# How the first gated per-layer input gets the low parts of its weights: a subtraction on GpSimd in place of a negative on ScalarE and an adding transfer

## The chip, the cores and the metric

The kernel runs on one core of a Trainium2 chip. The metric is the device time of one execution in microseconds, the median over several runs. Lower is better. The profile is one profiled execution, whose rows the prediction quotes.

## The reference

A two-layer decoder trunk over 512 tokens of 1024 features, all in float32. Each layer has a half-step SwiGLU, a token mixer (retention in layer 0, forgetting attention in layer 1), a second half-step SwiGLU, and then a gated per-layer input. The last of these is what the change touches:

```python
for i in range(DEPTH):
    nw = norm_w[i]
    h = h + 0.5 * swiglu(rmsnorm(h, nw[0]), ffn_w_in[i, 0], ffn_w_out[i, 0])
    hn = rmsnorm(h, nw[1])
    h = h + (retention(...) if i % N_MIXERS == 0 else forgetting_attention(...))
    h = h + 0.5 * swiglu(rmsnorm(h, nw[2]), ffn_w_in[i, 1], ffn_w_out[i, 1])
    gate = jax.nn.sigmoid(rmsnorm(h, nw[3]) @ ple_w_gate[i])
    h = h + gate * (p[i] @ ple_w_proj[i])
return rmsnorm(h, final_norm_w)
```

## The kernel before

The hidden state h lies in SBUF, transposed, as eight blocks of 128 features by 512 tokens. Every product is made of three TensorE products in a rounded type (fp32r): high part of the weight with high part of the input, high with low, low with high. TensorE's order is written out by hand; the order of the instructions on ScalarE (ACT), VectorE (DVE), GpSimd (POOL) and SyncE (SP, which issues the loads) is made by a planner from the program's order, its own durations and the buffers that are free. Each of these engines then works through its list in order.

**Weights.** All weight tiles stand in one list (W.plan). take() hands out the next one and first makes those up to two further ahead (LOOKAHEAD). A tile's making: SP loads 512 KB into one of four raw buffers (wraw); ScalarE copies it, rounded, to the tile's high half; the low half is raw minus high. There are three tiles (wpool), so a new one can only be written when TensorE has left an older one. For the low half there are two ways, chosen by W.low when a tile is made:

- an engine: ScalarE's copy (L82), then a subtraction on that engine (L83), VectorE's or GpSimd's;
- None: ScalarE's copy (L120), ScalarE's negative of the raw tile into the low half (L121), and a transfer that reads the weights from memory again and adds them to it (L122). The transfer is issued from GpSimd's queue, and the raw buffer is free after the negative.

The feed-forwards do most of their input weights in pairs (Strassen's scheme). Of a pair's quarters, sums are made on VectorE (L151) and split (L82, L83); the first half of a pair and one of its quarters get their low parts by negative and adding transfer whatever W.low is. The first two weight pairs of a feed-forward are done plainly (plain(), L524), and their halves are ordinary tiles of the list.

**The gated input, ple().** In layer 0 it is done in one part of 512 tokens (parts is 1), in layer 1 in two. For each of the eight blocks m there are a gate product (gates(), through proj() and mm3(), L312 to L314: 24 matmuls) and a projection (added(): 6 matmuls), each in a PSUM bank of its own. rest(m) then multiplies the gate by the norm's row (L1106, VectorE), takes the sigmoid (L1107, ScalarE), multiplies by the projection (L1110) and adds to h (L1111). nxt.block(m) follows: it prepares the block for the next feed-forward's norm, in quarters for the pairs (quarters(): scaled copies L381 and L396 and rounded parts L376 and L384 on ScalarE, differences L388, L406, L411, L412 and low parts L377 and L385 on VectorE; four more splits L305 and L306) and squares it (L428, L432).

The list is here: projection tile, five gates, the second projection tile, three gates, and then the next feed-forward's two plain pairs as four tiles. As tiles are made two ahead, the projection's first tile and the first gate are made before ple() sets W.low, and the feed-forward's first two tiles are made inside it, at the last two gates. W.low is set back to VectorE at the end of ple(). One projection tile is held over four blocks, so the gates have the other two tiles between them.

Of the kernel before, what the change touches and what calls it, by code (L numbers as in the profile page):

```python
# [187 lines left out]
def trunk(ctx, tc, a):  # L188
    nc = tc.nc
# [15 lines left out]
    W = Weights(tc, wraw, wpool)  # L205
# [81 lines left out]
    def bank():  # L287
        return psum.tile([P, S], F32, name="bank")

    def temp(dtype=F32):  # L290
        return tmp.tile([P, S], dtype, name="tmp")
# [19 lines left out]
    def mm3(out, wh, wl, xh, xl, first, last):  # L311
        nc.tensor.matmul(out, wh, xh, start=first, stop=False)  # L312
        nc.tensor.matmul(out, wh, xl, start=False, stop=False)  # L313
        nc.tensor.matmul(out, wl, xh, start=False, stop=last)  # L314
# [159 lines left out]
    def proj(srcs, n, out=None, cols=slice(0, S), take=W.take):  # L474

        ws = [take(s) for s in srcs]
        os = out or [bank() for _ in ws]
        for k in range(KB):
            ks = slice(k * P, (k + 1) * P)
            for o, (wh, wl) in zip(os, ws):  # L480
                mm3(o, wh[:, ks], wl[:, ks], n.hi[k][:, cols], n.lo[k][:, cols], k == 0, k == KB - 1)
        return os
# [581 lines left out]
    def ple(l, n, nxt, phi, plo, parts=1):  # L1064

        w = S // parts
        with ExitStack() as pools:
# [7 lines left out]
            def weights(src):  # L1075
                if id(src) not in ws:
                    ws[id(src)] = W.take(src)
                return ws[id(src)]

            for part in range(parts):  # L1080
                ts_ = slice(part * w, (part + 1) * w)

                both = {}

                def half(m, i):

                    if parts == 1:
                        return bank()
                    if m not in both:
                        both[m] = bank()  # L1090
                    return both[m][:, i * w : (i + 1) * w]

                def gates(ms):
                    return proj([ple_g[l][m] for m in ms], n, [half(m, 1) for m in ms], ts_, weights)

                def added(m):
                    wp = weights(ple_p[l][m // 4])
                    o = half(m, 0)
                    for k in range(2):
                        ks = slice(((m % 4) * 2 + k) * P, ((m % 4) * 2 + k + 1) * P)  # L1100
                        mm3(o, wp[0][:, ks], wp[1][:, ks], phi[k][:, ts_], plo[k][:, ts_], k == 0, k == 1)
                    return o

                def rest(m, g, o):
                    t1, t2, hm = temp()[:, :w], temp()[:, :w], h[m][:, ts_]
                    nc.vector.tensor_tensor(out=t1, in0=g, in1=n.r[:, ts_], op=ALU.mult)  # L1106
                    nc.scalar.activation(t1, t1, AF.Sigmoid)  # L1107
                    if parts > 1 and m == KB - 1:
                        nc.scalar.activation(warm, t1[:, 0:1], AF.Sqrt)
                    nc.vector.tensor_tensor(out=t2, in0=o, in1=t1, op=ALU.mult)  # L1110
                    nc.vector.tensor_tensor(out=hm, in0=hm, in1=t2, op=ALU.add)  # L1111
                    if parts == 1:
                        nxt.block(m)
                    else:
                        nxt.new = m == 0
                        nxt.square(m, ts_, keep=m == KB - 1)
                        nc.gpsimd.tensor_scalar(out=hm, in0=hm, scalar1=fw[:, m : m + 1], scalar2=None, op0=ALU.mult)

                m = 0
                if part == 0:  # L1120
                    W.low = None if parts == 1 else nc.gpsimd
                    os = [added(m) for m in range(2 + parts)]
                    gs = gates((0,)) if parts == 1 else gates((0, 1, 2, 3))
                    n.columns()
                    m = len(gs)
                    gs += gates((m,))
                    n.rows()
                    if parts == 1:
                        os += [added(3)]
                        rest(0, gs[0], os[0])  # L1130
                        gs += gates((2,))
                        rest(1, gs[1], os[1])
                        gs += gates((3,))
                    for m in range(2 if parts == 1 else 0, 4):
                        rest(m, gs[m], os[m])
                    m = 4
                    if parts > 1:
                        rest(4, gs[4], added(4))
                        m = 5
                while m < KB:  # L1140
                    g = gates((m,))[0]
                    rest(m, g, added(m))
                    if part > 0 and m == 2:
                        diag = final_scale(nxt, slice(ts_.start - w, ts_.start))
                    if part > 0 and m == 4:
                        final(diag, slice(ts_.start - w, ts_.start))
                    m += 1
# [4 lines left out]
    def final_scale(n, ts_):  # L1152

        w = ts_.stop - ts_.start
        nb = w // P
        totals = [bank() for _ in range(nb)]
        for i, t in enumerate((n.acc[:, ts_], n.kept)):
            for j in range(nb):
                nc.tensor.matmul(
                    totals[j][:, 0:2], t[:, j * P : (j + 1) * P], ones[:, 0:2], start=i == 0, stop=i == 1  # L1160
                )
        r, v, t = (stat.tile([P, nb], F32, name=x) for x in ("last", "cv2", "ct2"))
        for j in range(nb):
            mean_eps(v[:, j : j + 1], totals[j][:, 0:1])
        rsqrt(r, v, t)
        diag = temp()[:, :w]
        nc.vector.tensor_tensor(
            out=diag.rearrange("p (j t) -> p j t", j=nb), in0=ident.unsqueeze(1).to_broadcast([P, nb, P]),
            in1=r.unsqueeze(2).to_broadcast([P, nb, P]), op=ALU.mult,
        )  # L1170
        return diag

    def final(diag, ts_):
        w = ts_.stop - ts_.start
        rows, copy = bank()[:, :w], temp()[:, :w]
        nc.tensor.matmul(rows, ones, diag, start=True, stop=True)
        nc.scalar.copy(copy, rows)
        ov = a["outT"].rearrange("(b p) t -> p b t", p=P)
        for b in range(KB):
            hb = h[b][:, ts_]  # L1180
            if b < 2:
                nc.gpsimd.tensor_tensor(out=hb, in0=hb, in1=copy, op=ALU.mult)
            else:
                nc.vector.tensor_tensor(out=hb, in0=hb, in1=rows, op=ALU.mult)
        for b0, b1, eng in ((2, 4, nc.sync), (4, 6, nc.scalar), (0, 2, nc.scalar), (6, 8, nc.sync)):
            eng.dma_start(out=ov[:, b0:b1, ts_], in_=hall[:, b0:b1, ts_])
# [142 lines left out]
```

## Time and profile before

| | |
|---|---|
| median of 3 runs | 2228.97 us (2226.98 to 2231.87) |
| span of the profiled execution, first to last instruction | 2230.5 us |
| TensorE busy | 2154.5 us, 97% |
| VectorE, ScalarE, GpSimd busy | 1447.1, 1212.3, 450.7 us |
| moved by transfers | 272.33 MB |
| granted TensorE clock, mean | 0.987 |

Of the profiled execution the page gives the span; its own time from outside isn't listed apart from the three runs, and the span lies within their spread. The gated input of layer 0 runs from about 1126 to 1193 us of the span, the next feed-forward's plain part till about 1230.

How to read the rows. In a timeline a row is: start, duration, engine, line, operation, written tile and what it reads, shapes, count; in brackets the engine's idle time before it and what ended that. PE is TensorE, PEld its weight load; L12 is line 12 of the kernel. The end of a matmul is modelled: each row lasts longer than the distance to the next. A row of waits names who waited for whom: total us, times, longest. The chain that ended last is followed back from the end, and its rows are start, duration, what. In a row of windows stand the stretch, its length, then busy time and instructions of PE, PEld, DVE, ACT and POOL, granted clock, share of the transfer engines, GB/s. A row of transfers ends with KB each and us from issue to landing. A row of groups by tile or line gives count, shortest, median and longest in ns, and the first and last start.

### The profile page before, as it was taken

To read this page: it belongs to the slowest core of one execution; us is meant where nothing else is said; L and a number is where in the kernel's file an instruction comes from. 1 tells how busy PE (TensorE), PEld (TensorE's weight loads), DVE (VectorE), ACT (ScalarE), POOL (GpSimd) and SP (SyncE) were. 2 spreads that over 40 slices of the span, in tenths; PEclk is the share of its full clock that TensorE was granted. 3 is DMA by queue.
4 is the path that set the end of the run, shared out by engine and by line. 5 is a ranking of instruction groups with operands and counts; after the bars stand their busy time and mean duration, and the time that the engine had idled before them with its cause. 6 is when DMAs were issued, how large, how long until landed. Compare 5 with 4: busy or idle time off the path is not lost.

```text
span 2230.5 us, 34455 instructions
## 1 busy us (share of the span) xinstructions
PE 2154.5 (97%) x13525; PEld 1937.5 (87%) x13525; DVE 1447.1 (65%) x2631; ACT 1212.3 (54%) x2037; POOL 450.7 (20%) x352
## 2 busy tenths in 40 slices
PE   7999999999999999999997999999999999999998
PEld 7999997888888798989876989898788888999987
DVE  8686776352542776767746677675675686777764
ACT  7565553433233663735555646364786775555543
POOL 0010003444444010101110001012334200110154
PEclk9999999999999999999998999999999999999999
DMA  5465563232222254746464457373622244655631
GB/s 176 113 163 150 138 161 95 81 99 76 88 83 76 85 137 119 170 133 152 129 151 117 114 136 182 113 167 103 153 91 87 69 116 112 159 158 137 152 104 39
DMA packets 86755, 272.33 MB, mean 122 GB/s; under 512 B 9520, under 2 KB 13104, under 8 KB 86592
## 3 DMA queue, kind: packets, MB, share of 16 engines
q1 hardware_dynamic: 63328, 209.78, 28.7%
q0 software_dynamic: 22032, 59.25, 15.9%
q8 instruction: 106, 1.74, 0.3%
q10 hardware_dynamic: 1232, 1.09, 0.1%
q14 instruction: 57, 0.47, 0.1%
HBM read 267.96 MB, written 2.13 MB: 121 GB/s over the span
## 4 chain that ended last, share of the span: by engine, by line
PE 80%; DVE 7%; ACT 6%; DMA 4%; issue 3%; POOL 0%; SPq 0%; DVEq 0%; ACTq 0%; POOLq 0%
PE bank L493 29%; PE bank L314 14%; PE bank L312 13%; PE bank L313 13%; PE bank L524 3%; DMA wraw<-in_ffn_w_in 3%; PE bank L678 2%; PE bank L679 2%; PE bank L680 2%; DVE w L83 1%; DMA w<-in_ple_gate 1%; DVE sums L151 1%; ACT p L982 1%; ACT w L82 1%; DVE tlo L303 1%
## 5 line engine op out<-in xcount | busy, mean ns | idle before, releaser
L82 ACT CAST w<-wraw 128x1024 fp32r<-128x1024 f32 (+1 forms) x232 | 235.1, 1021 | 431.0 <-PE bank L314 252.6
L314 PE MATMUL bank<-unit_a,w 128*128 128x512 f32 x736 | 288.9, 393 | 12.7 <-DMA w<-in_ple_gate 8.4
L312 PE MATMUL bank<-unit_a,w 128*128 128x512 f32 x736 | 289.8, 394 | 1.9 <-ACT w L82 1.6
L313 PE MATMUL bank<-unit_a,w 128*128 128x512 f32 x736 | 287.9, 391 | 0.2 <-DVE unit_a L303 0.2
L82 ACT CAST s<-sums 128x512 fp32r<-128x512 f32 x320 | 191.2, 617 | 155.3 <-DVE sums L151 106.6
L314 PE MATMUL bank<-unit_d,w 128*128 128x512 f32 (+1 forms) x712 | 268.1, 377 | 4.6 <-DVE w L83 4.6
L312 PE MATMUL bank<-unit_d,w 128*128 128x512 f32 (+1 forms) x712 | 269.2, 378 | 3.2 <-ACT w L82 1.6
L313 PE MATMUL bank<-unit_d,w 128*128 128x512 f32 (+1 forms) x712 | 268.3, 377 | 1.8 <-DVE unit_d L303 1.8
L83 DVE TENSOR_TENSOR s<-sums,s 128x512 fp32r<-128x512 f32 x320 | 213.7, 686 | 81.4 <-ACT s L82 80.4
L83 POOL TENSOR_TENSOR w<-wraw,w 128x1024 fp32r<-128x1024 f32 x83 | 202.6, 2445 | 233.5 <-ACT w L82 223.4
L122 POOL DMA_DIRECT2D a<-in_ffn_w_in x80 | 70.1, 876 | 651.4 <-ACT a L121 444.8
L83 DVE TENSOR_TENSOR w<-wraw,w 128x1024 fp32r<-128x1024 f32 (+1 forms) x149 | 175.8, 1185 | 28.3 <-ACT w L82 27.7
L493 PE MATMUL bank<-unit_b,s 128*128 128x256 f32 x880 | 185.9, 278 | 0.0
L493 PE MATMUL bank<-unit_d,s 128*128 128x256 f32 x1140 | 179.2, 277 | 0.0
L314 PEld LDWEIGHTS bank<-unit_a,w 128*128 128x128 f32 x736 | 138.8, 189 | 45.5 <-DMA w<-in_ple_gate 10.1
L493 PE MATMUL bank<-unit_a,s 128*128 128x256 f32 x1260 | 176.1, 277 | 1.9 <-ACT unit_a L376 1.1
L585 DVE SCALAR_TENSOR_TENSOR tmp<-bank,rows 128x512 f32<-128x512 f32 x96 | 66.0, 689 | 165.3 <-PE bank L314 164.0
L312 PEld LDWEIGHTS bank<-unit_a,w 128*128 128x128 f32 x736 | 139.0, 189 | 32.4 <-ACT w L82 3.5
L313 PEld LDWEIGHTS bank<-unit_a,w 128*128 128x128 f32 x736 | 139.0, 189 | 28.8 <-DVE unit_a L303 0.5
L493 PEld LDWEIGHTS bank<-unit_a,s 128*128 128x128 f32 x1260 | 158.8, 188 | 2.7 <-ACT unit_a L376 1.6
L314 PEld LDWEIGHTS bank<-unit_d,w 128*128 128x128 f32 x712 | 134.4, 189 | 30.5 <-DVE w L83 6.6
L312 PEld LDWEIGHTS bank<-unit_d,w 128*128 128x128 f32 x712 | 134.5, 189 | 30.3 <-ACT w L82 3.3
(270 smaller groups left out, 4801.1 us busy)
## 6 DMA issues: line engine op xcount, KB each, us to landing
wraw<-in_ffn_w_in SPq DMA_DIRECT2D x174, 512.0 KB, 4.3
wraw<-in_ffn_w_out SPq DMA_DIRECT2D x64, 512.0 KB, 4.7
w<-in_ffn_w_in POOLq DMA_DIRECT2D x58, 512.0 KB, 5.5
a<-in_ffn_w_in POOLq DMA_DIRECT2D x80, 256.0 KB, 6.2
wraw<-in_ffn_w_out SPq DMA_DIRECT2D x32, 384.0 KB, 3.7
wraw<-in_ret_qk SPq DMA_DIRECT2D x16, 512.0 KB, 3.5
wraw<-in_ret_v SPq DMA_DIRECT2D x16, 512.0 KB, 3.6
wraw<-in_ret_g SPq DMA_DIRECT2D x16, 512.0 KB, 3.5
```

The lines of the kernel that those rows point to most:

```text
L82: self.nc.scalar.copy(hi, raw)
L83: self.low.tensor_tensor(out=lo, in0=raw, in1=hi.bitcast(F32), op=ALU.subtract)
L122: self.nc.gpsimd.dma_start(out=lo, in_=src, accum_op=ALU.add)
L312: nc.tensor.matmul(out, wh, xh, start=first, stop=False)
L313: nc.tensor.matmul(out, wh, xl, start=False, stop=False)
L314: nc.tensor.matmul(out, wl, xh, start=False, stop=last)
L493: add = lambda w, x, start, stop: nc.tensor.matmul(out, w, x, start=start, stop=stop, skip_group_check=True)
L524: nc.tensor.matmul(o[:, HALVES[t]], x[:, ks], y, start=k == t == q == 0, stop=k == KB - 1 and q == 2, skip_group_check=True,)
L585: nc.vector.scalar_tensor_tensor(out=t1, in0=o, scalar=-0.5, in1=n.r, op0=ALU.mult, op1=ALU.mult)
L678: nc.tensor.matmul(os[t], xh, wh[:, js], start=k == 0, stop=False)
L679: nc.tensor.matmul(os[t], xh, wl[:, js], start=False, stop=False)
L680: nc.tensor.matmul(os[t], xl, wh[:, js], start=False, stop=k == KB - 1)
```

## The change

One line of ple() changes. In the first part of the gated input W.low becomes GpSimd in both layers; in layer 1 it already was.

```diff
                 m = 0
                 if part == 0:
-                    W.low = None if parts == 1 else nc.gpsimd
+                    W.low = nc.gpsimd
                     os = [added(m) for m in range(2 + parts)]
```

For the tiles made while that holds in layer 0, split() goes from the second way to the first: no negative on ScalarE, no transfer issued from GpSimd's queue, but a subtraction of 128x1024 on GpSimd, which reads the raw buffer and the high half. The tiles, the matmuls and their order on TensorE stay.

## The prediction

> **What bounds the kernel now.** I read, in this order: the head of the page; what TensorE waits for around the first gated input (1095 to 1225 us); the timeline of each engine there; the chain that ended last in the same place.
>
> ```profile
> span 2230.5 us, 34455 instructions
> PE 2154.5 (97%) x13525; PEld 1937.5 (87%) x13525; DVE 1447.1 (65%) x2631; ACT 1212.3 (54%) x2037; POOL 450.7 (20%) x352
> PE bank L524 <- DMA w<-in_ffn_w_in: 9.3, 1, 9.3
> PE bank L314 <- DMA w<-in_ple_gate: 8.4, 4, 3.5
> ```
>
> TensorE bounds the program and idles for 76 us in all; 17.7 us of that are here, and both waits are for transfers that the change removes. Time can come only out of these idles or out of a slow clock, and be lost only as new idles. The timeline of TensorE shows the five gaps, of 0.47, 1.02, 3.37, 3.55 and 9.25 us:
>
> ```profile
> 1145.28 0.50 PE L314 MATMUL bank<-unit_a,w 128*128 128x512 f32 x1 [0.47 <-DMA w<-in_ple_gate]
> 1152.03 0.50 PE L314 MATMUL bank<-unit_a,w 128*128 128x512 f32 x1 [1.02 <-DMA w<-in_ple_gate]
> 1167.95 0.50 PE L314 MATMUL bank<-unit_a,w 128*128 128x512 f32 x1 [3.37 <-DMA w<-in_ple_gate]
> 1185.39 0.50 PE L314 MATMUL bank<-unit_a,w 128*128 128x512 f32 x1 [3.55 <-DMA w<-in_ple_gate]
> 1186.66 0.51 PE L313 MATMUL bank<-unit_a,w 128*128 128x512 f32 x1
> 1190.30 0.40 PE L313 MATMUL bank<-unit_a,w 128*128 128x512 f32 x1
> 1203.50 3.15 PE L524 MATMUL bank<-unit_b,w 128*128 128x256 f32 x13 [9.25 <-DMA w<-in_ffn_w_in]
> 1209.68 1.26 PE L524 MATMUL bank<-unit_c,w 128*128 128x256 f32 x6
> ```
>
> Between 1186.66 and 1190.30 ten matmuls take 3.64 us, where undisturbed ones start 0.227 apart (0.23 in the chain's rows below): the clock was halved after the 3.55 us gap, which costs 3.64 - 2.27 = 1.4 us. The rows from 1203.50 are half-rate too at first.
>
> The last gap is the largest, but the chain says that it isn't what sets the end of this place:
>
> ```profile
> 1191.85 0.23 PE bank L313
> ...
> 1192.34 1.05 ACT w L120
> ...
> 1199.13 0.62 ACT a L120
> 1199.75 0.54 ACT tmp L1107
> ...
> 1209.08 0.34 DVE tmp L412
> 1209.42 0.61 DVE unit_c L377
> 1210.03 0.04 issue
> 1210.08 1.94 PE bank L524 x14
> ```
>
> Here the reader sees ScalarE and VectorE, not the transfer: TensorE, released at 1203.50, reaches the norm's last block (unit_c) at 1209.68 and finds it just being split. Had the low part come at once, TensorE would still have stood at unit_c till 1210.0. So the 9.25 us gap alone is worth about 0.3 us. What starts that chain is the copy at 1192.34, which waits for gate 7 to leave its weight tile.
>
> **The change, part by part.** Which tiles: the ones emitted while W.low is None.
>
> ```profile
> L120 ACT CAST w<-wraw x10: 1042/1054/1057, 1126.7 to 1192.3; 128x1024 fp32r<-128x1024 f32 x10
> L121 ACT ACTIVATE w<-wraw x10: 1042/1048/1057, 1127.7 to 1193.9; 128x1024 fp32r<-128x1024 f32 x10
> 1192.34 1.05 ACT L120 CAST w<-wraw 128x1024 fp32r<-128x1024 f32 x1 [4.98 <-PE bank L314]
> 1195.25 0.87 POOL L122 DMA_DIRECT2D w<-in_ffn_w_in  x1 [11.39 <-ACT w L121]
> w<-in_ffn_w_in POOLq DMA_DIRECT2D x1, 512.0 KB, 8.2
> w<-in_ple_gate POOLq DMA_DIRECT2D x7, 512.0 KB, 7.3
> L83 POOL TENSOR_TENSOR w<-wraw,w x83: 2359/2392/3631, 367.8 to 2168.2; 128x1024 fp32r<-128x1024 f32 x83
> ```
>
> Ten tiles: seven gates, one projection, and the first two of the next feed-forward (call the last one B). Removed: ten negatives of 1.05 us on ScalarE, ten issues of 0.87 on GpSimd, ten adding transfers of 7 to 8 us. Added: ten subtractions of 2.39 us on GpSimd (up to 3.63 in disturbed places). The copies stay. From the copy's start to the low part in place: before, for B, 1195.25 + 8.2 - 1192.34 = 11.1 us; after, 1.05 + 2.39 = 3.4, at most 4.7.
>
> *Gate stalls: gone, -10.9 us.* A gate's tile comes free two weights earlier; TensorE then has a projection (6 matmuls), a gate (24) and a projection (6) before the third matmul of the tile, 36 x 0.227 = 8.2 us. 11.1 doesn't fit into that (3.37 and 3.55 missing), 4.7 does with 3.5 to spare for a copy late in ScalarE's queue. The gaps sum to 8.41; start to start each loses 0.16 more (a matmul's row lasts 0.39, the next starts after 0.227) and 0.11 in the restart (0.34 to the next), 4 x 0.27 = 1.1; and the half clock's 1.4 goes. Gate 7 then ends, and B's copy could start, at 1192.34 - 10.9 = 1181.4.
>
> *B's low part: 9.25 becomes about 2 us.* TensorE needs it some 2 us after gate 7 (a projection of 1.4, five matmuls); it comes 3.4 to 4.7 after. By the chain above this is covered by the norm: nothing.
>
> *What is late next: the elementwise chain, +4.8 us.* From B's copy to unit_c it takes 1210.03 - 1192.34 = 17.7 us, whatever TensorE does. It would move by the full -10.9 if VectorE kept up. But a VectorE instruction with both inputs in SBUF stands still beside a GpSimd subtraction, as the retention stage shows:
>
> ```profile
> 472.31 0.68 DVE L698 TENSOR_TENSOR tmp<-bank,sin 128x512 f32<-128x512 f32 x1
> 472.91 2.91 DVE L700 TENSOR_TENSOR tmp<-tmp 128x512 f32<-128x512 f32 x1
> 472.88 2.39 POOL L83 TENSOR_TENSOR w<-wraw,w 128x1024 fp32r<-128x1024 f32 x1 [0.69 <-ACT w L82]
> 1095.00:1193.00 98.00, 89.59 (x390) 72.84 (x389) 49.37 (x81) 53.13 (x77) 18.45 (x16) 0.98 0.55 135
> ```
>
> 2.91 for 0.68: 2.2 us lost to one subtraction; an instruction that reads a PSUM bank (L698) or falls into a gap loses nothing. So a subtraction costs the chain 0 to 2.2 us. The Trainium skill says the same on its page "SBUF — State Buffer", section "SBUF: two separate sides": VectorE with two SBUF inputs and GpSimd hold one pair of ports as an exclusive lock, for the whole instruction. The rows here agree with it; by that rule taken at its worst the change is the slow rival below.
>
> VectorE is half busy here (49.37 of 98 us), so the early subtractions (gates 2 to 6, the projection) I cost at nothing: the chain there waits for TensorE's banks, with ScalarE idle up to 4.98 ahead of a copy. Without that cover they would cost six times 0 to 2.2. The three of gate 7 and the two feed-forward tiles stand where VectorE next splits the norm's blocks from SBUF (L377, L388, L406): three times 1.6, between the half of 2.2 and the whole, is 4.8. The lowest is 0, the highest nine times 2.2 = 19.8. The first of the ten, at 1127.7, has the last squares' sum behind it on GpSimd, and after that:
>
> ```profile
> 1131.96 0.69 DVE L303 TENSOR_TENSOR tmp<-acc,tmp 128x512 fp32r<-128x512 f32 x1 [1.86 <-ACT tmp L302]
> 1135.97 0.95 PE L326 MATMUL bank<-ones_r,tmp 128*128 128x2 f32 x8
> ```
>
> 1135.97 - 1131.96 - 0.69 = 3.3 us of cover, against 2.39 - 0.87 = 1.5 more on GpSimd: nothing (without the cover 1.5).
>
> *ScalarE:* ten negatives gone, 10.5 us of 53 busy; off the chain but for the one at 1193.92, whose place the subtraction takes. *SP's queue:* a raw buffer comes free when the subtraction, no longer the negative, has read it. B's raw buffer carries the next pair's load, and ScalarE's L120 at 1199.13 waits for that:
>
> ```profile
> 1193.92 1.04 ACT L121 ACTIVATE w<-wraw 128x1024 fp32r<-128x1024 f32 x1
> 1194.99 4.12 DMA wraw<-in_ffn_w_in
> wraw<-in_ple_gate SPq DMA_DIRECT2D x16, 512.0 KB, 3.5
> 1201.10 0.88 POOL L122 DMA_DIRECT2D a<-in_ffn_w_in  x1 [4.97 <-ACT a L121]
> ```
>
> Free 3.4 us after the copy's start instead of 2.6: +0.9; the load without an adding transfer beside it 3.5 instead of 4.1: -0.6. I take +0.3; ends 0 and +0.9. *GpSimd's queue:* behind B's subtraction stands only the next pair's adding transfer, issued at 1201.10 before; nothing.
>
> *The clock, +1.7 us.* TensorE, early at unit_c, waits there in pieces for up to 10 us, and the row at 1186.66 shows what follows a gap of 3.55: 3.4 us at half rate, 1.7 lost. Before, the same loss (from 1203.50) lay under the chain. Ends: 0 (pieces too short) and 3.4 (two such stretches). The Trainium skill's page "TensorE: Matmul & The Clock Gate", section "Part 1: The HAM clock gate (the "warmup" mystery)", gives a free-running window of 3413 ns for it; the trace's 3.4 us agrees, and by that rule the term is one window, as taken.
>
> **Sum:** -10.9 + 4.8 + 0.3 + 1.7 = -4.1 us, against a span of 2230.5; the time outside the span isn't shown. The span lies 1.5 us above the median of the runs (2228.97), so the median becomes 2224.9, or 0.18% less. A measurement of this kernel tells about 0.2% (4.5 us) from no change: the forecast lies just at that edge.
>
> **Rivals.**
>
> ```profile
> 1231.04 1.23 DVE L83 TENSOR_TENSOR w<-wraw,w 128x1024 fp32r<-128x1024 f32 x1 [6.99 <-ACT w L82]
> ```
>
> *The norm keeps up, gain of 9 to 11.* Subtractions fall beside PSUM reads, or the planner, which orders ScalarE, VectorE and GpSimd anew, puts the pair sums (L151, L83, 4 to 5 us of VectorE inside the 17.7) behind the norm's last block. For it: half-busy VectorE. Against: the next stage has little to give, since the 6.99 us of idle VectorE in this row are the slack in which postponed sums can be made before the first block with pairs. -10.9 + 0.3 + 1.7 or less: 2218 to 2220.
>
> *Hidden anyway, no change.* The elementwise chain turns out to be paced by itself from gate 2 on: the early subtractions cost too, and together all nine take about 1 us each, 9.2 in all, which with 0.3 + 1.7 is the 10.9 that the gates gain. 2227 to 2231.
>
> ```profile
> 2155.15 6.21 POOL L83 TENSOR_TENSOR w<-wraw,w 128x1024 fp32r<-128x1024 f32 x2
> 2155.66 3.43 DVE L83 TENSOR_TENSOR w<-wraw,w 128x1024 fp32r<-128x1024 f32 x1
> ```
>
> *Slower: the shared ports.* All nine stand in VectorE's way, at 1.6 each: 14.4 + 0.3 + 1.7 - 10.9 = +5.5, 2234.5; at 2.2 each 2240. It decides from 1.0 us per subtraction on the chain. For it: in the last stage two subtractions beside a busy VectorE took 3.1 each (the first row), and VectorE's own 3.43 for the 1.23 of the row at 1231.04. Against: here VectorE has half its time free, and a late block only matters once TensorE has used up its banks.
>
> *Does it do what it says?* Yes: split() with GpSimd as W.low always subtracts; pairs keep their own adding transfers.
>
> **How the numbers follow.** Forecast 0.45 (its own range 2220 to 2229), norm keeps up 0.25, hidden 0.16, slower 0.14. Faster by over 0.2% (below 2224.5): the 0.25 and not quite half of the forecast's, 0.45; within 0.2%: 0.40; slower: the 0.14 and a little of what the new order may spoil elsewhere, 0.15. Range: from between the forecast and the full gain, 2216, to the slower rival's 2234; outside lie about 2 in 10.
>
> **What would show it.** Right: no wait for w<-in_ple_gate; ten more L83 subtractions on GpSimd at 2.4 to 3.1; gate 7 ends near 1181; TensorE's new wait before 1205 names VectorE's L377 or L385; VectorE's two-SBUF rows stretched to 1.5 to 2.9 from 1140 on; unit_c near 1204 to 1206. Wrong: TensorE still waiting for low parts (then copies are stuck in ScalarE's queue); unit_c at 1199 or before (locks cheap); waits in gates 3 to 7 for banks or copies (locks everywhere); or the difference arising after 1250, where the change touches nothing but the planner's order.

## The result, and the profile after

The changed kernel takes 2217.13 us (median of 4 runs, 2215.84 to 2218.95), the one before 2228.15 beside it: ratio 0.9944, 95% interval 0.9928 to 0.9961. Two repetitions gave 0.995 (0.9934 to 0.9966) and 0.9948 (0.9929 to 0.9968). Over all runs of this study the mean is 12.1 us lower (16 runs against 111, standard error 0.9). The forecast was -4.1.

The head of the profile after, and GpSimd's group of subtractions between 1110 and 1215 us:

```profile
span 2214.2 us, 34442 instructions
PE 2148.7 (97%) x13525; PEld 1933.3 (87%) x13525; DVE 1459.4 (66%) x2631; ACT 1203.1 (54%) x2027; POOL 466.8 (21%) x352
L83 POOL TENSOR_TENSOR w<-wraw,w 128x1024 fp32r<-128x1024 f32 x10 | 24.9, 2493 | 39.6 <-ACT w L82 35.6 <-issue 4.0
```

Ten subtractions of 2.5 us have come, ten negatives and ten adding transfers have gone. What TensorE waits for between 1095 and 1245 us:

```profile
PE bank L524 <- ACT w L82: 5.7, 1, 5.7
PE bank L524 <- POOL w L83: 2.4, 1, 2.4
PE bank L493 <- ACT tmp L545: 2.3, 1, 2.3
PE bank L524 <- ACT unit_c L376: 1.2, 1, 1.2
PE bank L524 <- DVE w L83: 0.7, 1, 0.7
PE bank L524 <- DVE unit_c L377: 0.4, 1, 0.4
```

No wait for a gate's weights is left. In their place stands one of 5.7 us for a copy that the forecast didn't have. TensorE's timeline there (start, duration, what, wait):

```profile
1182.17 0.51 PE L524 MATMUL bank<-unit_b,w 128*128 128x256 f32 x3
1188.34 0.80 PE L524 MATMUL bank<-unit_b,w 128*128 128x256 f32 x2 [5.66 <-ACT w L82]
1191.54 3.14 PE L524 MATMUL bank<-unit_b,w 128*128 128x256 f32 x13 [2.40 <-POOL w L83]
1199.88 0.38 PE L524 MATMUL bank<-unit_c,w 128*128 128x256 f32 x1 [1.18 <-ACT unit_c L376]
1200.69 0.86 PE L524 MATMUL bank<-unit_c,w 128*128 128x256 f32 x5 [0.43 <-DVE unit_c L377]
```

In the kernel before it was:

```profile
1193.50 0.75 PE L524 MATMUL bank<-unit_b,w 128*128 128x256 f32 x5
```

So the plain feed-forward starts 11.3 us earlier (1182.17 for 1193.50); unit_c is reached at 1199.88 instead of 1209.68. ScalarE's list tells why tile B is late, VectorE's what the locks do:

```profile
1182.70 0.72 ACT L396 ACTIVATE tmp<-hall,small 128x512 f32<-128x512 f32 x1 [3.06 <-DVE hall L1111]
1187.26 1.03 ACT L82 CAST w<-wraw 128x1024 fp32r<-128x1024 f32 x1
1165.88 2.79 DVE L1111 TENSOR_TENSOR hall<-hall,tmp 128x512 f32<-128x512 f32 x1
1179.87 2.80 DVE L1111 TENSOR_TENSOR hall<-hall,tmp 128x512 f32<-128x512 f32 x1
1189.20 2.58 DVE L306 SCALAR_TENSOR_TENSOR unit_a<-hall,small,unit_a 128x256 fp32r<-128x256 f32 x1
1199.95 0.69 DVE L377 TENSOR_TENSOR unit_c<-tmp,unit_c 128x512 fp32r<-128x512 f32 x1
```

Before, ScalarE stood 4.98 us at the copy of B (1192.34) with L396 of block 6 behind it. The planner has now put block 6's instructions (L396 at 1182.70) ahead of that copy, so the copy starts only at 1187.26, though gate 7 ended near 1180.8. VectorE's two-input rows of 0.69 and 0.48 us stretch to as much as 2.8 beside a subtraction; the excesses of its nine stretched rows sum to 12.1 us. Ahead of the first split of unit_c VectorE's list had seven sums and subtractions of the feed-forward's weights (L151, L83) before. The planner has now put three of them, pair sums of 1.8 us, behind it. Their rows, first in the kernel before (unit_c split at 1209.34), then after (split at 1199.95):

```profile
1202.12 1.29 DVE L83 TENSOR_TENSOR s<-sums,s 128x512 fp32r<-128x512 f32 x2
1207.13 0.68 DVE L151 TENSOR_TENSOR sums<-sums,wraw 128x512 f32<-128x512 f32 x1
1207.73 0.68 DVE L151 TENSOR_TENSOR sums<-wraw 128x512 f32<-128x512 f32 x1
1202.09 0.69 DVE L83 TENSOR_TENSOR s<-sums,s 128x512 fp32r<-128x512 f32 x1
1203.29 0.69 DVE L151 TENSOR_TENSOR sums<-sums,wraw 128x512 f32<-128x512 f32 x1
1203.89 0.68 DVE L151 TENSOR_TENSOR sums<-wraw 128x512 f32<-128x512 f32 x1
```

### The profile page after: what moved, and what is told of

It reads as the page before. It is cut to its first block, busy times and chain, and to the rows that moved or that the text cites. A ratio compares the mean times of both kernels' runs of the same rounds, so it can differ in the third digit from the quotient of the medians.

```text
span 2214.2 us, 34442 instructions
## 1 busy us (share of the span) xinstructions
PE 2148.7 (97%) x13525; PEld 1933.3 (87%) x13525; DVE 1459.4 (66%) x2631; ACT 1203.1 (54%) x2027; POOL 466.8 (21%) x352
## 4 chain that ended last, share of the span: by engine, by line
PE 81%; DVE 7%; ACT 5%; issue 4%; DMA 3%; POOL 1%; SPq 0%; DVEq 0%; ACTq 0%; POOLq 0%
PE bank L493 31%; PE bank L314 13%; PE bank L312 13%; PE bank L313 13%; PE bank L524 3%; DMA wraw<-in_ffn_w_in 2%; PE bank L678 2%; PE bank L679 2%; PE bank L680 2%; DVE w L83 1%; POOL w L83 1%; ACT p L982 1%; ACT w L82 1%; DVE sums L151 1%; DVE tlo L303 1%
## 5 line engine op out<-in xcount | busy, mean ns | idle before, releaser
L82 ACT CAST w<-wraw 128x1024 fp32r<-128x1024 f32 (+1 forms) x242 | 245.5, 1022 | 439.7 <-PE bank L314 257.3
L83 POOL TENSOR_TENSOR w<-wraw,w 128x1024 fp32r<-128x1024 f32 x93 | 226.5, 2439 | 273.7 <-ACT w L82 259.6
L83 DVE TENSOR_TENSOR s<-sums,s 128x512 fp32r<-128x512 f32 x320 | 213.8, 686 | 83.1 <-ACT s L82 82.0
L83 DVE TENSOR_TENSOR w<-wraw,w 128x1024 fp32r<-128x1024 f32 (+1 forms) x149 | 175.8, 1185 | 23.4 <-ACT w L82 23.3
```

Of the source, the lines that this page charges most:

```text
L82: self.nc.scalar.copy(hi, raw)
L83: self.low.tensor_tensor(out=lo, in0=raw, in1=hi.bitcast(F32), op=ALU.subtract)
```

## The experiments

All are compared in three ways. The mean of the times against the kernel before (111 runs; standard error in brackets). From each trace, matmul by matmul (TensorE's program is the same in all): the **stretch**, by how much the way from the matmul at 1062.1 to the one at 1221.6 us of the first profile changes (minus is shorter); and the **block**, by how much VectorE's first split of unit_c (L377) moves (minus is earlier), counted from the first of these two matmuls. Several traces of one kernel are separated by commas.

| kernel | ratio (95%) | mean time, us | stretch, us | block, us |
|---|---|---|---|---|
| before, again | 0.9999 (0.9988 to 1.0011) | 0 | 0.0 | 0.0 |
| after | 0.995, 0.9948 | -12.1 (0.9) | -9.3, -7.6, -7.7 | -9.0, -8.9, -8.9 |
| after, old order | 0.9951, 0.9955, 0.9955 | -10.6 (0.8) | -5.1, -5.5, -6.2 | -7.5, -7.8, -7.5 |
| before, new order | 0.9975 (0.9964 to 0.9987) | -5.5 (1.1) | -3.4 | -9.2 |
| gated input's eight tiles only | 0.9952, 0.9959 | -9.7 (1.0) | -4.6, -6.4 | -12.4, -12.4 |
| feed-forward's two tiles only | 1.0016 (1.0006 to 1.0026) | +5.8 (0.5) | +5.2 | +1.6 |
| VectorE subtracts | 0.9951 (0.9936 to 0.9967) | -12.1 (0.8) | -7.4 | -12.2 |
| GpSimd in halves | 0.9938 (0.9917 to 0.9959) | -15.3 (1.2) | -11.4 | -12.7 |
| pair sums late | 0.9943 (0.9929 to 0.9957) | -10.6 (1.0) | -8.3 | -11.3 |
| VectorE, sums late | 0.9964 (0.9952 to 0.9975) | -8.0 (0.6) | -4.9 | -14.3 |
| halves, B on VectorE, sums late | 0.9911, 0.9924 | -18.1 (1.0) | -13.4, -15.0 | -16.7, -16.8 |

**The two kernels again.** No edit.

> The changed kernel as it is, profiled and timed again. The two profiles so far differ by 16.3 us of span, the medians by 11.0. Theory A (the gates' gain less a norm that slows a little): what the change brings is the 9.0 us by which the norm's last block comes earlier; the rest of the 16.3 is in where the stretches of half clock fall, which differs between executions of one program. It expects a ratio of 0.994 to 0.996 and a second profile whose span is within 2 us of 2214 or up to 2218, with the block's split again near 1200.6 and stretches of half clock at other places after 1250 or none. Rival: the later gain belongs to the change (the order behind 1250 is better too): the second profile repeats the first to 0.5 us in every stretch, the ratio stays, and the kernel before repeats its own lost stretches in its second profile.

> The kernel before as it is, profiled and timed again. If the half-clock stretches at 1241.3, 1842.0 and 2159.5 us of its first profile depend on the execution, this profile lacks some of them or has others, and the span lies up to 5 us below 2230.5. If they belong to the program, they come again at the same places to 1 us, and the span is 2229 to 2231. Ratio 1.000, to 0.001.

> The changed kernel, profiled and timed a third time. So far, over 10 runs, its mean is 11.8 us below the kernel before's (74 runs); at one granted clock (1.76 us for each 0.001) 8.9 us remain, and 2.9 go with a mean clock of 0.9891 against 0.9875. If fewer half-clock stretches belong to the change (it takes four waits away, each of which can end in such a stretch), the clock is again 0.989 on the mean, and the difference at one clock 8 to 10 us. If they were luck, the clock is 0.9875 to 0.988 and the raw difference falls to 9 or less. The trace should show waits of 8 to 9.5 us between 1060 and 1231 again.

The stretch repeats to 1.6 us in three traces of the changed kernel, and the block to 0.1. From 1249 to 1486 us the traces of both kernels agree to 0.1 us, matmul by matmul. Elsewhere outside the stretch the same program differs from execution to execution: 111 runs of the kernel before spread with a standard deviation of 3.3 us. Two windows of 20 us at the same matmuls show how, one from each trace of the kernel before (start and end, length, busy times, and as third number from the end the granted clock):

```profile
1231.00:1251.00 20.00, 17.77 (x139) 17.57 (x138) 14.75 (x26) 14.30 (x25) 2.55 (x3) 0.91 0.46 105
1228.20:1248.20 20.00, 17.77 (x154) 17.58 (x154) 15.31 (x27) 15.44 (x27) 2.62 (x3) 1.00 0.52 124
```

The same wait of 2.2 us was followed by half clock in one execution (139 matmuls done, clock 0.91) and not in the other (154, clock 1.00). The two traces differ in the same way at 380 and 2160 us. So of the first pair of profiles, 16.3 us apart in span, only 9.3 lie in the stretch; the lost 1.6 us at 1241 and others were of the execution: the second trace of the kernel before doesn't have them. The third run of the changed kernel had a mean clock like the earlier ones: over 16 runs it is 0.9894, against 0.9875 in 111 of the kernel before.

**Change and order taken apart.** The changed kernel with the order that the kernel before has on ScalarE and VectorE, and the reverse. Edit, with the two lists of positions left out:

```diff
-        start(done)
+        start(done); i == 2 and pin(tc)
...
-        w = S // parts
+        w = S // parts; parts == 1 and MARK.append(len(nc.cur_bb.bb.instructions))
...
+def pin(tc):
+    for engine, order in ((mybir.EngineType.DVE, DVE_ORDER), (mybir.EngineType.Activation, ACT_ORDER)):
+        traced = [i for i in tc.nc.cur_bb.bb.instructions[MARK[0]:] if i.engine == engine]
+        for a, b in zip(order, order[1:]):
+            tc.add_manual_dep(traced[b], traced[a].name, ..., reason="pin")
```

> The changed kernel, but ScalarE and VectorE are held, in the stage of the first gated input, to the order that the kernel before has there (without its ten negatives). Theory A (the prediction's sum was right for the order it was made on; the planner's new order, with the pair sums behind the norm's last block, brought the rest): the norm's last block at 1203 to 1206 us instead of 1200.6, gain over before 4 to 7 us, ratio 0.997 to 0.998, 3 to 5 us slower than the changed kernel. Rival B (the order is immaterial, the locks on the chain are just cheaper than the 1.6 us that were put down): block at 1200 to 1201.5, ratio within 0.0007 of the changed kernel's. Rival C (the old order is better, since there the copy of the last weight tile comes right at gate 7's end): block at 1198 to 1200, 1 to 3 us faster than the changed kernel.

> The kernel before (negative on ScalarE and adding transfer), but ScalarE and VectorE are held, in the stage of the first gated input, to the order of the changed kernel. Theory A (order matters by the pair sums): the gates' waits stay, the last weight's low part comes later than before, since its copy stands further back on ScalarE, so TensorE waits 10 to 15 us ahead of the plain feed-forward; the norm's last block at 1208 to 1212, ratio 0.998 to 1.002: the order alone gives 2 to 3 us at the norm and loses some of it in the later copy. Rival B (order immaterial): ratio 0.9995 to 1.0005 and the block at 1210. If the order by itself gave most of the gain, the ratio would be 0.995 to 0.996 and the block near 1202.

TensorE and VectorE of the changed kernel in the old order:

```profile
1181.90 1.81 PE L524 MATMUL bank<-unit_b,w 128*128 128x256 f32 x13 [2.17 <-POOL w L83]
1191.60 0.58 PE L524 MATMUL bank<-unit_d,w 128*128 128x256 f32 x1 [5.74 <-ACT unit_d L384]
1196.93 0.58 PE L524 MATMUL bank<-unit_c,w 128*128 128x256 f32 x1 [2.88 <-ACT unit_c L376]
1199.20 1.48 PE L524 MATMUL bank<-unit_a,w 128*128 128x256 f32 x6
1197.23 0.68 DVE L377 TENSOR_TENSOR unit_c<-tmp,unit_c 128x512 fp32r<-128x512 f32 x1
```

B comes early here (1181.90), and TensorE stands at the norm's last two blocks instead, with half clock behind that: six matmuls take 1.48 where the full clock takes 0.88. The block is 7.5 to 7.8 us earlier, the stretch 5.1 to 6.2 shorter. In the kernel before with the new order:

```profile
1195.90 3.14 PE L524 MATMUL bank<-unit_b,w 128*128 128x256 f32 x13 [6.27 <-DMA w<-in_ffn_w_in]
1202.77 0.88 PE L524 MATMUL bank<-unit_c,w 128*128 128x256 f32 x6
1196.25 0.68 DVE L377 TENSOR_TENSOR unit_c<-tmp,unit_c 128x512 fp32r<-128x512 f32 x1
1180.54 0.71 ACT L396 ACTIVATE tmp<-hall,small 128x512 f32<-128x512 f32 x1
```

The order alone brings the block 9.2 us forward, as much as the whole change does, because L396 no longer stands behind a copy that waits for TensorE. But now the adding transfer ends the place: TensorE waits 6.27 us for it and comes to unit_c with no wait, 6.5 us after the block was split; 3.4 us are won. So there were two ends of nearly the same length, the elementwise list and the last low part, and taking away either one leaves the other. Theory A has the first kernel's gain in its stretch (4 to 7 us) but not in its time: a ratio of 0.997 to 0.998 was expected, and 0.9951 is within the 0.0007 of the changed kernel's that rival B, an immaterial order, had. In the second kernel it had TensorE's last wait as the end, though at 10 to 15 us, and it missed how far the order alone brings the block (it had 1208 to 1212 us; 9.2 earlier is about 1200). Over all runs the old order costs 1.5 us (standard error 1.1), less than the 2.6 of the traces. The kernel came twice more:

> The changed kernel with the order of the kernel before on ScalarE and VectorE, profiled and timed a second time. In its first trace TensorE's waits between 1060 and 1231 us were 4.3 us longer than in the changed kernel's two traces (13.0 against 8.7), yet its times were the changed kernel's to 1.5 us. If the order decides (theory A), the second trace repeats the long waits (12 to 14 us) and the times, brought to one granted clock with 1.76 us for each 0.001, lie 2 to 5 us above the changed kernel's. If the waits of the first trace were an accident of where TensorE's half-clock stretches fell (rival B), they are 8 to 11 us here and the times agree to 1.5 us.

> The changed kernel with the order of the kernel before, a third time. Two traces have the stretch 1060 to 1220 us 5.1 and 5.5 us shorter than before (the changed kernel: 7.6 to 9.3), with 13.7 us at half clock each; 16 times give 8.7 us at one clock, no less than the changed kernel's. If the order costs what the traces say, this trace has 4.5 to 6.5 us again and the pooled times move to 6 to 8 us. If the two profiled executions were unlucky in the clock, this one has less than 13 us at half clock in that place and 7 to 8.5 us.

The three stretches agree (5.1, 5.5, 6.2), so the order costs something there. How much of the time, between 0 and 3.5 us, stays open: with 1.8 us for each 0.001 of the granted clock (mean 0.9885 in these runs, 0.9894 in the changed kernel's) nothing is left of the 1.5.

**The two parts of the change.** A list of tiles that keep the old way:

```diff
-        if self.low is None and src is not None:
+        if src is not None and (self.low is None or id(src) in self.old):
...
-    plan_ffn(0)
+    W.old = [id(ffn_src[2][0][0].q), id(ffn_src[2][0][0].r)]; plan_ffn(0)        # gated input's eight tiles only
+    W.old = [id(x) for x in ple_g[0][1:] + ple_p[0][1:]]; plan_ffn(0)            # feed-forward's two only
```

The first two kernels listed two tiles too many each (the second plain pair; the first gate and projection), which VectorE had split until then:

> GpSimd subtracts for the eight tiles of the gated input alone; the two tiles of the plain feed-forward behind it keep the negative and the adding transfer. Compared by the time from 1060 us to 1250 us, in which the changed kernel's two profiles are 9.3 and 10.9 shorter than the first profile before. Theory A (the gates' waits are what was worth something; the 9.25 us ahead of the feed-forward lie beside the elementwise chain): the wait for the last low part stays, 8 to 12 us long, and that stretch is still 8 to 11 us shorter than before; two locks less on VectorE, two negatives more on ScalarE. Rival B (with the gates' waits gone the last low part becomes the end of the place, since its adding transfer starts 3.5 us after a copy that now stands further back on ScalarE): the plain feed-forward starts at 1198 or later and reaches the norm's last block after it was split, 3 to 5 us of the gain are lost, and the stretch is 4 to 7 us shorter than before.

> The other part alone: GpSimd subtracts for the two feed-forward tiles, the eight tiles of the gated input keep the negative and the adding transfer. Theory A (the last wait was worth 0.3 us): the gates' four waits stay (8.4 us in all), the 9.25 us wait shrinks to 1 to 3 us, TensorE then waits at the norm's last block instead, and the stretch from 1060 to 1250 is 0 to 2 us shorter than before; ratio 0.999 to 1.001. Rival B (the wait was worth its length): 5 to 9 us shorter, ratio 0.996 to 0.998.

They gave 1.0001 (0.9988 to 1.0015) and 1.0021 (1.0004 to 1.0038). In the first, TensorE waited another 7.57 us for one of the two extra tiles, which ate the gain. With the exact tiles:

> GpSimd's subtraction for the eight tiles of the gated input, and the old way for exactly the two feed-forward tiles that had it before (the earlier kernel of this kind also put two later tiles, VectorE's till then, on the old way, and TensorE waited 7.6 us for one of those). In that earlier trace TensorE waited 5.5 us for the last low part and still stood at the norm's last block 8.2 us earlier than before, counted from 1060 us. Theory A (the last low part is covered by the elementwise chain): block 8 to 9.5 us earlier, the stretch 1060 to 1250 shorter by 8 to 11, as in the changed kernel to 1.5 us, ratio 0.995 to 0.9965. Rival B (its lateness decides once the gates' waits are gone): 3 to 6 shorter, ratio 0.997 to 0.9985.

> GpSimd's subtraction for the eight tiles of the gated input only, a second time. Its first trace had the stretch 1060 to 1220 us 4.6 us shorter than before, its times were 7.3 us shorter at one clock. If the late low parts of the two feed-forward tiles cost what the first trace says (waits of 8.1 and 4.6 us for them, 9.9 in all with the others' floor taken off, against 8.7 in the changed kernel, and more half-clock after them), it stays 1 to 4 us behind the changed kernel at one clock; if that was an accident, within 1 us.

> GpSimd's subtraction for the two feed-forward tiles, and the old way for exactly the eight tiles of the gated input that had it before (the earlier kernel of this kind put two more tiles on the old way). Theory A: the gates' waits of 8.4 us stay, the 9.25 us one shrinks to 1 to 3, the stretch 1060 to 1250 is within 2 us of before, ratio 0.999 to 1.001. Rival B (the last wait was worth its length): 5 to 9 shorter. Rival C (the planner's order for this mix, not the waits, decides: in the earlier kernel the norm's last block came 4 us later than before although the feed-forward started 4 us earlier): 2 to 5 longer, ratio 1.001 to 1.0025.

The gated input's eight tiles alone, TensorE and VectorE:

```profile
1187.51 1.01 PE L524 MATMUL bank<-unit_b,w 128*128 128x256 f32 x3 [8.07 <-DMA w<-in_ffn_w_in]
1193.13 3.14 PE L524 MATMUL bank<-unit_b,w 128*128 128x256 f32 x13 [4.61 <-DMA w<-in_ffn_w_in]
1193.58 0.68 DVE L377 TENSOR_TENSOR unit_c<-tmp,unit_c 128x512 fp32r<-128x512 f32 x1
```

The block is split 12.4 us earlier, 3.5 more than in the changed kernel, and TensorE is still waiting for low parts by transfer: rival B in the first trace's stretch, though the ratio is theory A's. With the gates' waits gone, these two transfers are worth 2 to 3 us of the stretch; before, they lay beside the elementwise list. In the times they are worth 2.4 us (standard error 1.3), of which 0.7 is left at one granted clock. The feed-forward's two tiles alone make the kernel slower:

```profile
1190.13 1.06 ACT L82 CAST w<-wraw 128x1024 fp32r<-128x1024 f32 x1 [2.90 <-PE bank L314]
1191.74 2.45 DVE L377 TENSOR_TENSOR unit_d<-tmp,unit_d 128x512 fp32r<-128x512 f32 x1 [2.73 <-ACT unit_d L376]
1198.85 0.69 DVE L151 TENSOR_TENSOR sums<-wraw 128x512 f32<-128x512 f32 x1 [2.20 <-DMA wraw<-in_ffn_w_in]
1199.46 0.42 DVE L388 TENSOR_TENSOR tmp<-tmp 128x256 f32<-128x256 f32 x1
1206.01 0.58 PE L524 MATMUL bank<-unit_c,w 128*128 128x256 f32 x1 [4.38 <-ACT unit_c L376]
```

Here the planner put the copy of B ahead of a norm copy (L376) on ScalarE, and a pair sum (L151) that waits for its load ahead of L388 on VectorE: the norm stands 2.73 and 2.20 us in line behind instructions that aren't its own. TensorE starts the feed-forward sooner and waits 4.38 us for unit_c. That is rival C. The parts don't add up: -9.7 and +5.8 alone, -12.1 together.

**Without locks.** VectorE does the ten subtractions: `W.low = nc.vector if parts == 1 else nc.gpsimd`.

> The ten low parts by a subtraction on VectorE (1.2 us each) in place of GpSimd: no adding transfer, no lock, but 12 us more work on VectorE. In the changed kernel's trace VectorE's rows beside the ten GpSimd subtractions are longer than undisturbed ones by 10.3 us in all. Theory A (the locks charge VectorE what its own subtraction would): the gates' waits are gone, and the norm's last block comes within 1.5 us of the changed kernel's; the stretch from 1060 to 1250 is 7.5 to 11 us shorter than before. Rival B (most of the stretch lies where VectorE would have waited anyway, and GpSimd takes 12 us off the chain): the block comes 3 to 7 us later than in the changed kernel, the stretch is 3 to 6 us shorter than before. Rival C (VectorE's own work falls into its waits, the locks do not): 1 to 2 us earlier than in the changed kernel.

VectorE's group between 1110 and 1215 us (five of the fifteen were VectorE's in both kernels), and TensorE:

```profile
L83 DVE TENSOR_TENSOR w<-wraw,w 128x1024 fp32r<-128x1024 f32 x15 | 18.3, 1222 | 5.6 <-ACT w L82 5.6
1188.09 0.58 PE L524 MATMUL bank<-unit_d,w 128*128 128x256 f32 x1 [4.21 <-ACT unit_d L384]
```

The time and the mean stretch are the changed kernel's to 1 us (theory A), although VectorE has 12 us more to do. That 1.22 us of its own work cost no more than a lock fits this but isn't shown by it: the planner dealt the lists out anew here too, with six of the seven weight sums and subtractions ahead of unit_c again, and no run takes the two apart. The block even comes 3.3 us earlier, which theory A didn't have; the wait of 4.21 us at the norm's block before it (unit_d) takes that back. The Trainium skill's "GPSIMD Engine Reference", section "3.1 Elementwise — side-by-side cycle accounting", gives an addition of two float32 tiles as 1.96 times slower on GpSimd; 2.39 against 1.22 us here is the same ratio.

**Shorter locks.** Each GpSimd subtraction as two of 512 columns (the lines that set `cut` in ple() are left out):

```diff
-        self.low.tensor_tensor(out=lo, in0=raw, in1=hi.bitcast(F32), op=ALU.subtract)
+        [self.low.tensor_tensor(out=lo[:, c], in0=raw[:, c], in1=hi.bitcast(F32)[:, c], op=ALU.subtract) for c in ((slice(0, 512), slice(512, 1024)) if self.cut > 1 and src is not None else (slice(None),))]
```

> The changed kernel with each of the ten subtractions as two of 512 columns. If a VectorE instruction waits for the end of the one GpSimd instruction that runs, the single stretches fall from at most 2.2 us to at most 1.2, and VectorE gets a turn between the halves: theory A then expects the stretched rows to sum to 5 to 8 us instead of 10.3, and the norm's last block 1 to 2 us earlier. Rival B (two locks cost together what one cost, since VectorE meets the second half too): the sum stays at 9 to 12 us and the block where it was, to 1 us. The subtraction itself should take some 2 x 1.25 us.

```profile
L83 POOL TENSOR_TENSOR w<-wraw,w 128x512 fp32r<-128x512 f32 x20 | 29.4, 1491 | 32.0 <-ACT w L82 28.1 <-issue 3.9
1183.65 1.49 DVE L306 SCALAR_TENSOR_TENSOR unit_a<-hall,small,unit_a 128x256 fp32r<-128x256 f32 x1
1185.07 1.48 DVE L388 TENSOR_TENSOR tmp<-tmp 128x256 f32<-128x256 f32 x1
```

GpSimd needs 29.4 us in place of 24.9, but the excess of VectorE's stretched rows falls from 12.1 to 7.2 us and no row is stretched by more than 1.1. The block comes 3.8 us earlier than in the changed kernel, more than theory A's 1 to 2. ScalarE and VectorE have the changed kernel's order here up to unit_c, so no new order has a part in it. VectorE gets its turn when the running GpSimd instruction ends: in the changed kernel L1111 of 1179.87 ends at 1182.67, 0.55 us behind the subtraction of 1179.72 to 1182.12. The Trainium skill states the lock as one for the whole instruction ("SBUF — State Buffer", section "SBUF: two separate sides"); this trace agrees, and shows that a shorter instruction costs less.

**Pair sums behind the norm.** The changed kernel's own order, pinned as above, with VectorE's L83, L151, L151, L83 moved behind the last split of unit_c, and ScalarE's copies for them too; then the same with VectorE's subtractions; then with halves and tile B on VectorE.

> The changed kernel with its own order on ScalarE and VectorE, except that VectorE's first pair sums and one weight subtraction (L83, L151, L151, L83: 3.3 us ahead of the norm's last block) are held behind that block, and the copies that go with them on ScalarE. Theory A (VectorE's busy time ends the place, the locks are part of it): the block is split 2.5 to 4 us earlier, the stretch 1060 to 1250 gets 1.5 to 3 us shorter than the changed kernel's, because TensorE comes to the block itself only at the start of the plain feed-forward plus 13 + 24 matmuls. Rival B (TensorE at the block is bound by the last low part, not by VectorE): less than 0.7 us shorter. Rival C (the sums are then late for the first pair): a new wait at the first matmuls on s, 1 us or more, and no gain.

> All ten subtractions on VectorE (no lock at all), and the pair sums held behind the norm's last block on VectorE and ScalarE. With the planner's order the first of these was 10.6 us below the kernel before at one granted clock, and TensorE then stood 4.2 and 2.8 us ahead of the norm's last two blocks behind sums of 4 us. Theory A (what ends the place is VectorE's busy time ahead of the last block, whoever fills it): the block is split 3 to 5 us earlier than in that kernel, 12.5 to 15 us below before at one clock, as the version with halves (13.2). Rival B (GpSimd's help is worth something in itself, 10 us less on VectorE): 10 to 12 us, behind the version with halves.

> Three things on top of the change: each GpSimd subtraction in two halves, the last tile's subtraction (L83) on VectorE for 1.2 us in place of GpSimd's 3.1 to 3.4, and the pair sums held behind the norm's last block as in the kernel before this one. Theory A: TensorE starts the plain feed-forward about 2 us earlier than the changed kernel, meets the block without a wait of more than 1 us, and the stretch 1060 to 1250 is 13 to 16 us shorter than in the first profile before; ratio 0.992 to 0.994. Rival: another bound shows at once (the load of the next raw tile, or the sums for the first pair), and it stays at the changed kernel's 0.995.

> The version with halves, the last subtraction on VectorE and the pair sums behind the norm, a second time, to narrow its interval: so far 0.9911, and 12.9 us below the kernel before at one granted clock. Expected 0.9905 to 0.9935, 11.5 to 14.5 us at one clock; waits of TensorE between 1060 and 1231 of 5 to 6 us. Were the first ratio luck of the clock, it would come to 0.9935 to 0.995.

With the sums late the block comes 2.4 us earlier, close to theory A's 2.5 to 4, but the time doesn't move: what was won at unit_c is lost at the next tile (the wait below is new), much as rival C had it, though at another place. With VectorE's subtractions it is lost several times over:

```profile
1206.08 0.50 PE L524 MATMUL bank<-unit_b,w 128*128 128x256 f32 x2 [1.42 <-ACT w L82]
1206.83 0.80 PE L524 MATMUL bank<-unit_b,w 128*128 128x256 f32 x2 [6.12 <-ACT w L82]
1204.69 0.62 ACT L120 CAST a<-wraw 128x512 fp32r<-128x512 f32 x1 [4.20 <-DMA wraw<-in_ffn_w_in]
```

The first row is the changed kernel with late sums; the other two are VectorE's subtractions with late sums: there the weight copy that TensorE waits 6.12 us for stands in ScalarE's list behind a pair's copy (L120) that waits 4.20 for a load. Both theories on that kernel missed this; the kernel says nothing on the locks. In the third kernel the lists fit:

```profile
1179.89 0.50 PE L524 MATMUL bank<-unit_b,w 128*128 128x256 f32 x2 [1.99 <-ACT w L82]
1182.42 2.78 PE L524 MATMUL bank<-unit_b,w 128*128 128x256 f32 x13 [2.02 <-DVE w L83]
1198.11 0.50 PE L524 MATMUL bank<-unit_b,w 128*128 128x256 f32 x2 [1.75 <-ACT w L82]
1199.37 2.69 PE L524 MATMUL bank<-unit_b,w 128*128 128x256 f32 x13 [0.76 <-DVE w L83]
1187.76 0.68 DVE L377 TENSOR_TENSOR unit_c<-tmp,unit_c 128x512 fp32r<-128x512 f32 x1
```

TensorE doesn't wait for the norm at all; what is left are the copy and the subtraction after a tile comes free, 4.0 us ahead of the first plain pair and 2.5 ahead of the second. This version beats both kernels: 0.9911 (0.9894 to 0.9929) and 0.9924 (0.9905 to 0.9942), 18.1 us.

## Why the prediction was wrong, point by point

- *Gates, -10.9.* Right. Up to the matmul at 1190.5 us the three traces of the changed kernel gain 11.0 each, and no gate waits. One count in the working is off: between 1186.66 and 1190.30 there are nine matmuls, not ten, so the half clock there cost 1.6 us instead of 1.4 and the term comes to 11.1.
- *B's low part, covered, about 2 us.* The 2.40 us behind the copy are there. The 5.66 us ahead of it are not in the working: it let the copy start when gate 7 ends (1181.4), and it came at 1187.26. That a wait here was worth 0.3 us held only beside the other waits: with the gates mended it is worth 2 to 3 of the stretch (gated input's tiles only).
- *What is late next, +4.8: the step that failed.* The place was named rightly, its size was not. With the raw buffer's 0.3 the block was to fall 5.1 us behind the gates' gain; it fell 2.0 behind (8.9 of 11.0). The last three subtractions do stretch VectorE's rows, by 1.05, 2.1 and 2.1 us, 5.3 in all for the 4.8. But the tail, which "takes 17.7 us, whatever TensorE does", wasn't bare work to which that adds: counted the same way, from B's copy to the end of unit_c's split, it is now 13.4 (1187.26 to 1200.64). With the old order, on which the working was done, the block falls 3.4 to 3.8 us behind the gates' 11.2, although the last three rows are stretched by 5.2 there too; so about 1.5 us of the locks fell into waits. The other 1.5 or so came by the planner's new order, with 1.8 us of pair sums now behind unit_c's split.
- *Early subtractions, nothing.* Right: they stretch VectorE's rows (2.79 at 1165.88), and the gates don't feel it.
- *Raw buffer +0.3, ScalarE's negatives, GpSimd's queue.* No run tells these from nothing.
- *Clock, +1.7.* From the block to the end of the stretch 0.8 us were lost on the mean of three traces. The long wait comes early (5.66 us at 1182 to 1188), and the half clock is over when TensorE reaches unit_c (0.86 for five matmuls). In the old order the loss came as forecast (1.48 for 0.88), and the stretch of -5.1 to -6.2 lies near the -4.1 worked out.
- *Nothing outside this place: failed too, cause open.* The stretch gives -8.2 on the mean, the times -12.1. The mean clock of the runs rose from 0.9875 to 0.9894; over all runs of all kernels 0.001 of it goes with 1.8 us, so 3.4 us go with the clock, of which the stretch, matmul by matmul, holds about 0.6. That the change causes the rest (it takes away four waits, each of which could be followed by half clock) is argued, not shown. It fits that every kernel of the table without the gates' waits gained 2.3 to 5.0 us more time than stretch, the old order 5.0, while the feed-forward's two tiles alone, which keep all four, gained none. Against it, the stretch of the kernel before is known from two traces only.

So of the 8.0 us between the forecast (-4.1) and the mean (-12.1), 3.1 are the tail, 0.9 the clock in the stretch, and 3.9 lie outside it.

The rival that came nearest is "the norm keeps up" (2218 to 2220 for 2217.13 measured). Part of its reason holds: three of the pair sums went behind the norm's last block. But the block stayed 2.0 us behind the gates, and with the sums ahead of it again the time is nearly as low, so that its time came out is in part luck: it had nothing outside the stretch either. Its argument against, that the next stage has little to give, is true of the changed kernel with late sums and didn't matter. In the rival "hidden anyway" the sum is off: 9.2 + 0.3 + 1.7 is 11.2, not 10.9.

## What to carry to other kernels

A tail measured between two instructions is not work: go through each engine's list in it and ask which instruction stands behind another's wait, since a planner will deal these out anew after any edit. Where two things end a place at nearly the same time, the parts of a change don't add, and a part alone can even lose; try them together before judging one. Here it paid to cut GpSimd's subtractions beside VectorE in halves (3.2 us less than the changed kernel, standard error 1.5), and the fastest version also made the last one before a deadline on VectorE.

## What the runs showed of the hardware

- After a wait of 2.2 to 3.6 us TensorE's clock may or may not be halved, by execution (of the gates' two longest waits, 3.2 to 3.6 us, the second was followed by half clock in one trace of the kernel before and the first in the other). In each trace the changes of the granted clock lie multiples of 3.413 us apart, but where they lie against the program differs (the first half-clock stretch begins 20.5 to 23.6 us after the first matmul). The Trainium skill, "TensorE: Matmul & The Clock Gate", section "Part 1: The HAM clock gate (the "warmup" mystery)", calls the window free-running and its effect at a kernel's start run-variable; these traces agree and show it in mid-kernel. The 111 runs of the kernel before spread by a standard deviation of 3.3 us, most of which goes with their mean clock (0.984 to 0.991), so a single pair of profiles can't size a change of 10.
- Two half GpSimd subtractions cost 2.98 us against 2.49 for a whole one, and yet the kernel gained, by shorter stretches of VectorE.
